# Pacing the top-k rounds of a sparse-attention indexer: two per group of products in place of four in three groups

## The chip, the cores and the metric

The kernel runs on one core of one Trainium2 chip. The metric is the device time of one execution in microseconds. The median of three runs is 1857.63 us (1857.12 to 1858.28).

## What is computed

Two layers of a causal decoder trunk on 512 tokens of width 1024, in float32. Each layer has a mixer with three branches and a convolutional GeGLU. Branch A is a dilated window attention, B an attention over the keys that an indexer selects, C a differential attention of four heads. All three start from one projection; gates weigh them, and an output projection follows. Only the indexer matters here:

```python
logits = jnp.einsum('bqhd,bsd->bqhs', qib, k_idx)
score = jnp.einsum('bqhs,bqh->bqs', jax.nn.relu(logits), wb) * (IDX_DIM ** -0.5)
score = jnp.where(kpos[None, None, :] <= qpos[None, :, None], score, -jnp.inf)
_, idx = lax.top_k(score, topk)          # topk = 128 of 512 keys
```

B then attends over the selected keys alone. For the first 128 queries every causal key is selected, so only three tiles of 128 queries need a selection, over 256, 384 and 512 keys.

## The kernel before

TensorE works in float32 split into a high and a low part, so every product is three matmuls (`mm3`, lines 88 to 90). Weights come in by DMA on SP's queue into `wr`, ScalarE casts the high part `wh` (line 81), VectorE subtracts to get the low part `wl` (line 82). There are two `wr` buffers and five each of `wh` and `wl`; the loader runs one or two units ahead (`w_ahead`).

The mixer is written as a sequence of units in the list `ORDER`: projections of A and the indexer, then C heads 0 to 2, the gates `ga` 0 to 3, C head 3, `ga` 4 to 7, B, and the remaining gates. A unit of A, B or C has four tiles of products, and after each tile the function `slot()` (line 328) is called once. So a **group** below is one block of products and the call of `slot()` that stands behind it, numbered from 1 in each layer. A call emits, in this order: work that came due, two of the 24 indexer score jobs while there are any, the stages of the attention chains that are in flight (S: scores and softmax on lines 470 and 472, T: transposes and their split on lines 477 and 81/82, V: the product with the values on line 488), and last the top-k steps.

A **round** of top-k (`topk`, line 742) takes an 8-wide buffer `m8` (tag "s"), finds the eight largest scores of each row (MAX8, line 745) and replaces them with a mark (MATCH_REPLACE8, line 746, with a small load of the match values). There are 16 rounds for each of the three tiles, and a closing TENSOR_SCALAR on line 748 turns the marks into a mask. All of it runs on VectorE. Below, T1.1 to T1.16 are the rounds of the tile with 256 keys (its scores lie in the buffer `m`), T2.1 to T2.16 those with 384 keys and T3.1 to T3.16 those with 512 (both in `u`). A step that finds a tile finished takes the place of a round.

Seen in the order in which the code emits it (layer 0): T1.1 is in group 12, T1.13 in 21. In group 22 the function `combine_a` (lines 596 to 616) joins the first pair of A's outputs; it takes three "s" buffers, on lines 599, 605 and 606, and stands ahead of T1.14. T1.16 is in group 23, T2.1 in 25, T2.11 in 32. The three chains of C head 0 start in groups 33, 34 and 35. Each takes "s" buffers for the row minima (line 470) and for `r2` (line 675), and stands ahead of the rounds of its group: T2.12 in 33, T2.13 in 34 (the second `combine_a` is in that group as well), T2.14 and T2.15 in 35. T2.16 is in 36. The chains of C head 1 start in 37, 38 and 39, and T3.1 and T3.2 are in 38, T3.3 in 39, T3.16 in 49. `chains_b`, which needs the masks, is called in group 57; it runs all steps that are left first. In layer 1 the counter `tick` starts with what layer 0 left in it.

The tag "s" has 20 buffers (line 41), handed out by a framework that also decides, from its own simulated time, in which order each engine gets its instructions: an instruction that is ready while its engine is free may overtake work that was emitted earlier.

Of the kernel before, what the change touches and what calls it, by code (L numbers as in the profile page):

```python
# [49 lines left out]
def tile_trunk(ctx, tc, x, positions, w_in, w_br_a, w_br_b, w_br_c, w_out, lam_q1, lam_k1, lam_q2, lam_k2,  # L50
# [269 lines left out]
    fly = [None, None]  # L320
    score_jobs = []
    topk_steps = []
    tick = [0]

    def later(f, lag=1):
        pending.append([lag, f])
# [1 line left out]
    def slot():  # L328
        now = []
        for e in list(pending):  # L330
            e[0] -= 1
            if e[0] <= 0:
                pending.remove(e)
                now.append(e[1])
        for f in now:
            f()
        for _ in range(2):
            if score_jobs:
                score_jobs.pop(0)()
        c0 = chains.pop(0) if chains else None  # L340
        c1, c2 = fly
        if c1 is not None:
            c1.T()
        if c0 is not None:
            c0.S()
        if c2 is not None:
            c2.V()
        fly[0], fly[1] = c0, c1
        if topk_steps:
            tick[0] += 4  # L350
            while tick[0] >= 3 and topk_steps:
                tick[0] -= 3
                if next(topk_steps[0], None) is None:
                    topk_steps.pop(0)

    def rope(v, nh, t0, nt=1):
# [42 lines left out]
    def proj_unit(l, u, perm, nh, idx=None):  # L399
# [8 lines left out]
        for t in range(NT):  # L408
            units = w_get(keys)
            acc = proj_tile(units, t, n)  # L410
            w_ahead(2)
            nc.scalar.copy(qr[:, t], acc[:, 0:384])
            if perm is not None:
                nc.sync.dma_start(perm[t * P:(t + 1) * P, :], qr[:, t, 256:384])
            if idx is not None:
                nc.scalar.copy(idx["kr"][:, t, 0:HD], acc[:, 384:448])
                nc.scalar.activation(idx["w"][:, t, :], acc[:, 448:456], AF.Copy, scale=float(8 ** -0.5))
            if t < NT - 1:
                slot()
# [285 lines left out]
    def index_q(l, qi):  # L705
        keys = [(l, "I", kk) for kk in range(4)]
        for t in range(1, NT):
            units = w_get(keys)
            acc = proj_tile(units, t, 512)
            w_ahead(2)  # L710
            qr = alloc([P, 512], F32, "sm")
            nc.scalar.copy(qr, acc)
            rope(heads(qr.unsqueeze(1)), 8, t)

            def go(t=t, qr=qr):
                tp = palloc("tp")
                for b in range(4):
                    nc.tensor.transpose(tp[:, b * P:(b + 1) * P], qr[:, b * P:(b + 1) * P], ident)
                c = slice((t - 1) * P, t * P)
                stack_q(qi[:, 0:8:2, c], qi[:, 1:8:2, c], tp.rearrange("p (b c) -> p b c", b=4))  # L720
            later(go, 2)
            if t < NT - 1:
                slot()
# [28 lines left out]
    def branch(l, gi, c0, c1, oTs, ys, first_term):  # L752
        kt = len(oTs)
        cpu = 8 // kt
        for c in range(c0, c1):
            wg, wb = w_get([(l, "gate", gi, c), (l, "br", gi, c0, c // cpu)])
            acc = palloc("mm")
            for k in range(KT):
                mm3(acc, (wg[0][:, k], wg[1][:, k]), (xh[:, k], xl[:, k]), k == 0, k == KT - 1)
            w_ahead(2)  # L760
            th = alloc([P, S], F32, "th")
            nc.scalar.activation(th, acc, AF.Tanh, scale=0.5)
            pb = palloc("mm")
            cs = slice((c % cpu) * P, (c % cpu + 1) * P)
            for k in range(kt):
                mm3(pb, (wb[0][:, k, cs], wb[1][:, k, cs]), (oTs[k][:, 0], oTs[k][:, 1]), k == 0, k == kt - 1)
            y = ys[c // 2][:, c % 2]
            if first_term:
                nc.vector.scalar_tensor_tensor(y, th, 1.0, pb, op0=ALU.add, op1=ALU.mult)
            else:  # L770
                nc.vector.scalar_tensor_tensor(th, th, 1.0, pb, op0=ALU.add, op1=ALU.mult)
                nc.vector.tensor_tensor(y, y, th, op=ALU.add)
            slot()
            yield c
# [265 lines left out]
```

## Time and profile before

| | |
|---|---|
| median of three runs | 1857.63 us |
| the profiled execution, its own time | 1860.71 us |
| its span, first to last instruction | 1858.9 us |
| instructions | 25416 |
| TensorE (PE) busy | 1834.1 us |
| VectorE (DVE) busy | 1155.1 us |
| ScalarE (ACT) busy | 867.7 us |
| mean granted TensorE clock | 0.996 |

The profile covers one execution. PE is matmuls, PEld weight loads, DVE VectorE, ACT ScalarE, POOL GpSimd, SP the queue that issues the DMAs. Times in the rows are us from the start of the span, means are ns. L745 is line 745 of the code. A granted clock of 1.00 is 2.4 GHz and one of 0.50 is 1.2 GHz; a value between is the mean over a stretch.

### The profile page before, as it was taken

How to read it: one execution, taken by the hardware profiler on the slowest of the kernel's cores; microseconds unless marked ns; L12 is line 12 of the kernel's file. 1: busy time of each engine (PE TensorE's matmuls, PEld its weight loads, DVE VectorE, ACT ScalarE, POOL GpSimd, SP SyncE). 2: the span in 40 equal slices, each digit the busy share in tenths (PEclk: the TensorE clock that was granted, in tenths of full speed). 3: DMA queues.
4: the chain of work that ended last, by engine and by line, in shares of the span. 5: the costliest groups of instructions: out<-in, count | busy, mean ns of one | idle time of the engine just before them, and what ended most of it. 6: DMA issues, size and time to landing. Idle time of an engine off the chain costs nothing.

```text
span 1858.9 us, 25416 instructions
## 1 busy us (share of the span) xinstructions
PE 1834.1 (99%) x9565; PEld 1607.4 (86%) x9565; DVE 1155.1 (62%) x2138; ACT 867.7 (47%) x1518; POOL 28.3 (2%) x53
## 2 busy tenths in 40 slices
PE   8999999999999999999999999999999999999998
PEld 6999989988889888888889999789888798888886
DVE  6687798665457666642367787885545566666332
ACT  5665654463335444432256756545533354444221
POOL 0000000000000000000000000000000000000000
PEclk9999999999999999999999999999999999999999
DMA  5333323233343333333433333232332443332241
GB/s 162 90 80 101 85 66 84 70 91 90 104 143 121 105 102 91 96 100 126 127 105 84 80 99 89 78 79 77 97 98 86 149 123 98 103 94 91 102 152 64
DMA packets 265173, 185.22 MB, mean 100 GB/s; under 512 B 14710, under 2 KB 238298, under 8 KB 265050
## 3 DMA queue, kind: packets, MB, share of 16 engines
q1 hardware_dynamic: 265050, 183.60, 33.8%
q8 instruction: 75, 1.23, 0.3%
q14 instruction: 48, 0.39, 0.1%
HBM read 171.99 MB, written 11.57 MB: 99 GB/s over the span
## 4 chain that ended last, share of the span: by engine, by line
PE 67%; issue 20%; DVE 7%; DMA 3%; ACT 2%; SPq 1%; POOL 0%; DVEq 0%; POOLq 0%; ACTq 0%
PE mm L88 16%; PE mm L89 16%; PE mm L90 16%; PE sc L88 2%; PE sc L89 2%; PE sc L90 2%; PE pv L488 2%; PE sc L396 1%; PE sc L397 1%; PE tp L477 1%; DMA wr<-in_w_in_dram 1%; DVE wl L82 1%; PE pv L89 1%; PE pv L88 1%; PE pv L90 1%
## 5 line engine op out<-in xcount | busy, mean ns | idle before, releaser
L82 DVE TENSOR_TENSOR wl<-wr,wh 128x1024 fp32r<-128x1024 f32 (+2 forms) x314 | 359.1, 1146 | 369.5 <-ACT wh L81 368.6
L81 ACT CAST wh<-wr 128x1024 fp32r<-128x1024 f32 (+2 forms) x314 | 309.4, 989 | 458.0 <-PE mm L90 135.5
L88 PE MATMUL mm<-xh,wh 128*128 128x512 f32 (+1 forms) x784 | 297.6, 380 | 1.3 <-ACT xh L81 0.8
L89 PE MATMUL mm<-xl,wh 128*128 128x512 f32 (+1 forms) x784 | 297.3, 379 | 0.0
L90 PE MATMUL mm<-xh,wl 128*128 128x512 f32 (+1 forms) x784 | 297.2, 379 | 0.0
L89 PE MATMUL mm<-wl,xh 128*128 128x384 f32 (+2 forms) x816 | 283.0, 348 | 0.9 <-DVE wl L82 0.9
L90 PE MATMUL mm<-wh,xl 128*128 128x384 f32 (+2 forms) x816 | 283.6, 348 | 0.0
L88 PE MATMUL mm<-wh,xh 128*128 128x384 f32 (+2 forms) x816 | 281.5, 348 | 1.3 <-ACT xh L81 0.7
L88 PEld LDWEIGHTS mm<-xh,wh 128*128 128x128 f32 x784 | 147.9, 189 | 27.8 <-ACT xh L81 1.2
L89 PEld LDWEIGHTS mm<-xl,wh 128*128 128x128 f32 x784 | 147.7, 188 | 26.2 <-DVE xl L82 0.4
L90 PEld LDWEIGHTS mm<-xh,wl 128*128 128x128 f32 x784 | 147.8, 188 | 26.1
L89 PEld LDWEIGHTS mm<-wl,xh 128*128 128x128 f32 x816 | 154.4, 189 | 5.7 <-DVE wl L82 1.9
L88 PEld LDWEIGHTS mm<-wh,xh 128*128 128x128 f32 x816 | 154.4, 189 | 5.7 <-ACT xh L81 1.7
L90 PEld LDWEIGHTS mm<-wh,xl 128*128 128x128 f32 x816 | 154.4, 189 | 4.0 <-DVE s L226 0.3
L90 PE MATMUL sc<-xh,wl 128*128 128x512 f32 (+1 forms) x272 | 99.2, 365 | 0.0
L89 PE MATMUL sc<-xl,wh 128*128 128x512 f32 (+1 forms) x272 | 99.0, 364 | 0.0
L88 PE MATMUL sc<-xh,wh 128*128 128x512 f32 (+1 forms) x272 | 98.8, 364 | 0.0
L88 PE MATMUL mm<-wh,qk 128*128 128x512 f32 x216 | 85.8, 397 | 0.0
L89 PE MATMUL mm<-wl,qk 128*128 128x512 f32 x216 | 85.4, 396 | 0.0
L90 PE MATMUL mm<-wh,qk 128*128 128x512 f32 x216 | 85.1, 396 | 0.0
L488 PE MATMUL pv<-v,pt 128*128 128x128 f32 (+1 forms) x280 | 71.2, 297 | 2.7 <-ACT pt L81 2.7
L472 ACT ACTIVATE sm<-sm,s 128x128 f32<-128x128 f32 (+2 forms) x96 | 53.5, 558 | 43.3 <-DVE s L470 43.1
(274 smaller groups left out, 3251.8 us busy)
## 6 DMA issues: line engine op xcount, KB each, us to landing
wr<-in_w_ffn_up_dram SPq DMA_DIRECT2D x176, 256.0 KB, 3.4
wr<-in_w_in_dram SPq DMA_DIRECT2D x282, 128.0 KB, 2.5
wr<-in_w_in_dram SPq DMA_DIRECT2D x56, 512.0 KB, 3.9
wr<-in_w_ffn_down_dram SPq DMA_DIRECT2D x44, 512.0 KB, 3.7
wr<-in_w_out_dram SPq DMA_DIRECT2D x16, 512.0 KB, 3.6
xd<-u SPq DMA_DIRECT2D x12, 512.0 KB, 3.7
u<-xd SPq DMA_DIRECT2D x12, 512.0 KB, 5.2
u<-in_x_dram SPq DMA_DIRECT2D x8, 512.0 KB, 5.9
```

Source lines behind the costliest of these rows:

```text
L81: nc.scalar.copy(hi, src)
L82: nc.vector.tensor_tensor(lo, src, hi.bitcast(F32), op=ALU.subtract)
L88: nc.tensor.matmul(dst, a[0], b[0], start=start, stop=False)
L89: nc.tensor.matmul(dst, a[0], b[1], start=False, stop=False)
L90: nc.tensor.matmul(dst, a[1], b[0], start=False, stop=stop)
L396: nc.tensor.matmul(dst, q, kh, start=True, stop=False)
L397: nc.tensor.matmul(dst, q, kl, start=False, stop=True)
L472: nc.scalar.activation(e, e, AF.Exp, bias=mneg, scale=-1.0, accum_out=dcol)
L477: nc.tensor.transpose(tp[:, b * P:(b + 1) * P], e[:, b * P:(b + 1) * P], ident)
L488: nc.tensor.matmul(dst, pT[0][:, c], v, start=i == 0, stop=False)
```

## The change

In `slot()` the counter `tick`, which gives four steps to three calls (one, one, two), is replaced by a loop that takes two steps in every call. Nothing else differs: the rounds, their widths and the chains are the same.

```diff
     topk_steps = []
-    tick = [0]
...
         if topk_steps:
-            tick[0] += 4
-            while tick[0] >= 3 and topk_steps:
-                tick[0] -= 3
-                if next(topk_steps[0], None) is None:
+            for _ in range(2):
+                if topk_steps and next(topk_steps[0], None) is None:
                     topk_steps.pop(0)
```

## Rows read from the trace of the kernel before

**Rows 1.** From the page: busy time of the engines over the whole span (share, number of instructions).

```profile
PE 1834.1 (99%) x9565; PEld 1607.4 (86%) x9565; DVE 1155.1 (62%) x2138; ACT 867.7 (47%) x1518; POOL 28.3 (2%) x53
```

**Rows 2.** The windows view: stretch and its length, busy time (and instructions) of PE, PEld, DVE, ACT and POOL, the granted TensorE clock, the busy share of the DMA engines, GB/s. The first row is from layer 0, the second from layer 1.

```profile
240.00:270.00 30.00, 27.82 (x147) 23.94 (x146) 28.86 (x70) 20.10 (x39) 1.02 (x1) 0.94 0.36 89
...
1170.00:1200.00 30.00, 27.05 (x124) 21.96 (x124) 25.51 (x63) 15.57 (x35) 1.02 (x1) 0.89 0.24 65
```

**Rows 3.** The chain of work that ended last, in layer 1 between 1176 and 1186 us: start, us, what.

```profile
1177.32 0.61 DVE s L745
...
1178.44 0.75 DVE u L746 x2
...
1181.75 0.59 DVE s L745
...
1183.12 0.48 DVE pt L82
...
1183.64 0.47 PE pv L489
```

**Rows 4.** The same chain in layer 0 between 260 and 267 us.

```profile
262.68 0.59 DVE s L745
...
264.51 0.66 DVE u L746
...
265.84 0.87 PE tp L477 x3
```

**Rows 5.** VectorE's instructions by line and shape over the whole span: count, busy us, mean ns of one, idle time before them.

```profile
L745 DVE MAX8 s<-u 128x8 f32<-128x512 f32 x32 | 21.9, 684 | 0.1
...
L746 DVE MATCH_REPLACE8 u<-s,u 128x512 f32<-128x512 f32 x32 | 21.6, 676 | 0.0
...
L745 DVE MAX8 s<-u 128x8 f32<-128x384 f32 x32 | 17.7, 553 | 0.3
L746 DVE MATCH_REPLACE8 u<-s,u 128x384 f32<-128x384 f32 x32 | 17.4, 543 | 0.0
...
L745 DVE MAX8 s<-m 128x8 f32<-128x256 f32 x32 | 13.6, 424 | 0.5
L746 DVE MATCH_REPLACE8 m<-s,m 128x256 f32<-128x256 f32 x32 | 13.1, 408 | 0.0
...
L746 DVE MATCH_VALUE_LOAD u<-s,u 128x8 f32 x64 | 5.6, 87 | 0.7
```

**Rows 6.** The timeline of VectorE in layer 0: start, us, engine, line, operation, out<-in. The MAX8 at 116.68 is that of T1.13; the next ones shown are those of T1.14, T2.11, T2.12, T2.13 and T3.2.

```profile
116.68 0.41 DVE L745 MAX8 s<-m 128x8 f32<-128x256 f32 x1
...
164.17 0.16 DVE L606 TENSOR_TENSOR s<-md,u 128x8 f32<-128x8 f32 x1
164.25 0.42 DVE L745 MAX8 s<-m 128x8 f32<-128x256 f32 x1
...
194.46 0.56 DVE L745 MAX8 s<-u 128x8 f32<-128x384 f32 x1
...
221.83 0.16 DVE L675 RECIPROCAL s<-s 128x2 f32<-128x2 f32 x1
221.91 0.54 DVE L745 MAX8 s<-u 128x8 f32<-128x384 f32 x1
...
234.56 0.55 DVE L745 MAX8 s<-u 128x8 f32<-128x384 f32 x1
235.03 0.67 DVE L470 CUSTOM_DVE_ANT_0 sm<-sc,cmask 128x512 f32<-128x512 f32 x1
...
265.61 0.69 DVE L745 MAX8 s<-u 128x8 f32<-128x512 f32 x1
266.22 0.67 DVE L470 CUSTOM_DVE_ANT_0 sm<-sc,cmask 128x512 f32<-128x512 f32 x1
```

**Rows 7.** The windows view of VectorE alone (stretch, length, busy time, instructions, granted clock, DMA share, GB/s): the stretch that ends where the first `combine_a` has taken its buffers, and the one from there to the end of the last wait of PE nearby; layer 0, then layer 1.

```profile
91.00:164.20 73.20, 57.64 (x143) 1.00 0.33 87
164.20:266.80 102.60, 85.95 (x218) 0.99 0.34 87
1009.00:1080.30 71.30, 56.38 (x143) 1.00 0.32 84
1080.30:1185.00 104.70, 88.71 (x221) 0.99 0.35 91
```

**Rows 8.** The windows view of the top-k lines alone (same columns), after those stretches: line 745 (first two rows), line 746 (next two), line 748 (last two), each time layer 0 and layer 1.

```profile
266.80:346.00 79.20, 9.58 (x14) 0.99 0.27 69
1185.00:1256.00 71.00, 9.29 (x14) 0.96 0.25 66
...
266.80:346.00 79.20, 11.26 (x30) 0.99 0.27 69
1185.00:1256.00 71.00, 10.51 (x28) 0.96 0.25 66
...
266.80:346.00 79.20, 0.42 (x1) 0.99 0.27 69
1185.00:1256.00 71.00, 0.43 (x1) 0.96 0.25 66
```

**Rows 9.** The windows view of all engines (columns as in Rows 2) in the two stretches where the rounds T1.1 to T1.13 stand closest.

```profile
91.00:117.20 26.20, 26.20 (x153) 25.98 (x153) 24.87 (x63) 16.95 (x32) 0.00 (x0) 1.00 0.31 79
...
1009.50:1037.00 27.50, 27.50 (x163) 27.28 (x162) 25.93 (x66) 17.17 (x33) 0.00 (x0) 1.00 0.30 81
```

## The prediction

> **What bounds the kernel now.** I read the page first. TensorE is busy for 1834.1 of 1858.9 us, VectorE for 62% [rows 1]. The change adds and removes no instruction, it moves the rounds of one VectorE loop to earlier places. So it can only move the 24.8 us in which TensorE is idle, and the time that it spends at the lower clock. Next I looked in the windows view for where TensorE idles in the part that the change touches. There is one place per layer that matters, at the passage from C's projections to the first gates: 2.18 of 30 us idle in layer 0 (30.00 less 27.82), 2.95 in layer 1 [rows 2]. In both the granted clock falls behind the idle time: its mean is 0.94 and 0.89, which is 30 x 0.06 = 1.8 and 30 x 0.11 = 3.3 us of full speed not granted, one of the two levels being half. The rest of TensorE's idle time lies mostly at the start and the end, out of reach.
>
> Third, the chain of waits says what those places wait for. In layer 1 it runs through VectorE, and three pieces of it are top-k: 0.61, 0.75 and 0.59 us, ahead of the split of `pt` on line 82 that TensorE's product waits for [rows 3]. In layer 0 there are two, 0.59 and 0.66 us [rows 4]. VectorE is not the bound of the kernel, but it is the bound of this place.
>
> Last, the timeline shows what decides where a round runs, and it is not only the group in which it is emitted. T1.13 runs at 116.68 us, well ahead of its group; then no round runs for 47 us, and T1.14 follows at 164.25, directly behind line 606, the third "s" buffer of `combine_a` [rows 6]. T1.14 is exactly the first round that the code emits behind `combine_a`. T2.11 runs at 194.46, T2.12 waits until 221.91, directly behind line 675 of C head 0, behind which it is emitted. So the "s" buffers are handed out in program order: rounds run ahead as filler until the next "s" user that isn't ready. It holds the other way round too: line 470 of head 0's third chain comes directly behind the MAX8 of T2.13 (234.56, 235.03), and that of head 1's third chain directly behind T3.2 (265.61, 266.22) [rows 6]. A chain of C can't start its softmax before every round emitted ahead of it has its buffer.
>
> **The change, part by part.** A round of 512 columns costs 684 + 676 + 87 = 1447 ns, of 384 columns 553 + 543 + 87 = 1183 ns, of 256 columns 424 + 408 + 87 = 919 ns [rows 5]. I counted the emission again with two steps per call: T1.16 is in group 19, T2.3 in 21, `combine_a` in 22 as before, T2.16 in 28, T3.8 in 32, T3.10 in 33, T3.12 in 34, T3.14 in 35, T3.16 in 36, where it was 49.
>
> *Ahead of `combine_a`.* T1.14 to T1.16 and T2.1 to T2.3 become free to run in the stretch that ends at 164.2 us: 3 x 0.92 + 3 x 1.18 = 6.3 us more, where VectorE idles for 73.2 less 57.64 = 15.6 us; in layer 1 for 14.9 [rows 7]. TensorE has no wait there. I cost it at nothing; the cover is that idle time, and if it failed the price would be the 6.3 us.
>
> *From there to TensorE's wait.* All of T3 now has to run before head 1's first chain, so what stood behind 266.8 us comes forward: 9.58 + 11.26 + 0.42 = 21.3 us in layer 0, 9.29 + 10.51 + 0.43 = 20.2 in layer 1 [rows 8]. Out of the stretch go the 6.3 us just counted (in layer 1 5.4, since its counter starts one round further on). Net 15.0 and 14.8 us more. VectorE idles there for 102.6 less 85.95 = 16.65 us, and for 104.7 less 88.71 = 16.0 us [rows 7]. Left after the change: 1.65 and 1.2 us, under 2%. How full can it get? The fullest stretches, with rounds at hand as filler all the time, still leave 26.2 less 24.87 = 1.33 us (5.1%) and 1.57 us (5.7%) [rows 9]. At these shares 5.2 us of 102.6 and 6.0 of 104.7 stay unfilled, so VectorE overruns by 5.2 less 1.65 = 3.6 us and 6.0 less 1.2 = 4.8 us, 8.4 us together. What of it reaches TensorE no row settles. Nothing, if what is late is work for later units: behind the stretch 21 us of VectorE come free. All, if it is the chains of C. In the stretches of [rows 9] VectorE was 94 to 95% busy and TensorE lost nothing; in the 30 us to 270 it was 96% busy and TensorE lost 2.18 us [rows 2]. One of each kind: I take half, 4.2 us.
>
> *The chains of C.* Ahead of head 0's third chain there is now a round of T3 and the MAX8 of the next, 1.45 + 0.68 = 2.1 us, in place of the MAX8 of T2.13, 0.55 us: 1.6 us later on a piece that was on the path [rows 5, 6]. Head 0's second chain gets the same. Against it stand the rounds that leave the last few us before TensorE's wait, 1.25 us in layer 0 and 1.95 in layer 1 [rows 3, 4]. The two nearly cancel, and both are inside the VectorE sum above, so I add nothing.
>
> *The clock.* The wait stays where it is and the clock falls as before: 0 on the sum. Bounds: both falls gone, 1.8 + 3.3 = 5.1 us less; one more fall of 1.8 us in each layer, 3.6 us more.
>
> *Behind the stretch.* VectorE is relieved of 21 us, but TensorE has no wait there that the windows show, so it gains nothing. The masks are needed only in group 57, long after. No DMA is moved; SP and POOL keep their order, except that a late `wl` gives its `wr` back later, which is in the overrun.
>
> Sum: +4.2 us. The profiled execution (1860.71 us, 1.8 us of it around the span, 3.1 above the median) would become 1864.9, the median 1857.63 + 4.2 = **1861.8 us**.
>
> One rule of the Trainium skill speaks against the forecast: "Perfetto Trace Analysis", section "Identifying the Most-Contended Engine", names the engine with the highest occupancy as the one to work on, and for VectorE takes occupancy as a fair measure. At 62% the move would cost nothing and the sum would be 0. The same page's section "Optimization Strategy" adds that kernels can have regimes in which another engine is the contended one; the windows of this trace agree with that (96% of VectorE in the 30 us to 270).
>
> **The rivals.** *A: filler stays filler, no change.* TensorE's matmuls do not depend on the rounds, the buffers hold weights one or two units ahead, and it lost nothing at 95% of VectorE [rows 9]. The rounds already run ahead of their groups, so the new pace changes little of what VectorE does when. Then the overrun falls on later work and the time is 1857.6, give or take 2. Against it: the order of the "s" buffers makes the rounds a condition for the chains of C. That the change does nothing because the buffers, not the pace, place the rounds would look the same; but the counted emission moves rounds past those users, so I hold it for a part of this case only.
>
> *B: faster.* The waits at the passage to the gates are made by the top-k rounds inside them. With T3 finished by about 255 us these rounds are gone, and the chain gets 1.25 + 1.95 = 3.2 us shorter; the idle time before the falls of the clock shrinks and with it half of their cost, 2.6 us. That is 5.8 us less: 1851.8. It decides for itself if T3.16 is through before head 1's first chain needs it, and if the overrun stays under 1.25 us. For it: the pieces of [rows 3, 4] are directly ahead of the wait. Against it: under 2% of idle time is left in the 100 us before.
>
> *C: all of the overrun lands on TensorE.* 8.4 us and another fall of the clock per layer, 3.6: +12, 1869.6. For it: the path already runs through VectorE there. It is the far end of my own case.
>
> **How the numbers follow.** A difference of 0.2%, 3.7 us, is about what a measurement of this kernel can tell from no change. My case, from +2 us to the far end C, holds 0.48; a part of it lies under 3.7 us. Rival A holds 0.30, rival B 0.22. So slower by over 0.2%: 0.41; within: 0.37 (A and the small end of my case); faster: 0.22 (B). My case alone gives 1859.5 to 1869.6. The range for 8 in 10 goes from 1852.8, which takes in half of B, to 1868.5, which leaves out the tip of C.
>
> **What would show it.** In the changed profile T1.16 should run before about 130 us, T2.4 should follow line 606 of the first `combine_a`, T3.9 line 675 of head 0's first chain, and T3.16 should stand ahead of line 470 of head 1's first chain, by 255 us. No top-k should stand behind 266 us or 1185 us. VectorE should be at 96 to 99% from 164 to 267 us and from 1080 to 1185. If I am right, TensorE's idle time in the two passages grows from 5.1 us to 7 to 13 us, or new waits on `wl`, `pt` and `sm` appear from 195 us on. If that idle time shrinks and no new wait appears, B is right and the step that failed is the share of the overrun that reaches TensorE. If the rounds don't keep to this order of "s" buffers, the count of what moves is wrong.

## The result: 1.3% slower, behind the predicted range

| | before | after |
|---|---|---|
| median of four runs each, same chip | 1857.38 us | 1882.8 us (1880.57 to 1884.07) |
| the profiled execution, its own time | 1860.71 us | 1882.3 us |
| its span | 1858.9 us | 1880.5 us |
| mean granted TensorE clock | 0.996 | 0.993 |

The ratio is 1.0130, with an interval of 1.0118 to 1.0143: 25 us slower, where 4 were forecast and the range ended at 1868.5. The sign was right, the size was not.

From the page after, the line of [rows 1]:

```profile
PE 1844.8 (98%) x9565; PEld 1610.2 (86%) x9565; DVE 1158.6 (62%) x2138; ACT 866.8 (46%) x1518; POOL 28.1 (1%) x53
```

The same instructions run, and VectorE is still at 62%. TensorE's idle time goes from 24.8 to 35.7 us. Where it lies, the windows view tells. First the kernel before, then the one after, over the two passages of [rows 2] made wide enough to hold them in both (columns as there):

```profile
240.00:290.00 50.00, 47.82 (x254) 41.46 (x253) 43.59 (x105) 30.47 (x61) 1.16 (x2) 0.97 0.29 75
1170.00:1220.00 50.00, 47.05 (x239) 40.84 (x239) 41.70 (x107) 25.65 (x60) 2.12 (x2) 0.93 0.23 61
```

```profile
240.00:290.00 50.00, 42.51 (x219) 35.47 (x218) 43.69 (x107) 31.08 (x66) 1.02 (x1) 0.93 0.21 53
1170.00:1220.00 50.00, 43.40 (x201) 35.75 (x200) 42.58 (x100) 29.81 (x61) 1.02 (x1) 0.83 0.21 53
```

Idle time in the two passages: 2.18 + 2.95 = 5.1 us before, 7.49 + 6.60 = 14.1 after. Full speed not granted: 50 x (0.03 + 0.07) = 5.0 us before, 50 x (0.07 + 0.17) = 12.0 after. That is 9.0 + 7.0 = 16.0 of the 21.6 us between the spans, and the page's idle time adds 1.9 from elsewhere. Some 3.7 us are in matmuls that show as busy and stay unplaced. Outside the passages little is lost: layer 1's first block of products ends 10.5 us later than before, and around the second passage another 11 us are added.

What TensorE waits for there, in layer 0 and then in layer 1 (waits of PE: its operation and line, the releaser, us, times, longest). First the longest wait in the kernel before, then the waits after:

```profile
PE pv L489 <- DVE pt L82: 0.9, 1, 0.9
...
PE pv L489 <- DVE pt L82: 1.3, 1, 1.3
```

```profile
PE sc L393 <- DVE s L467: 2.6, 1, 2.6
PE pv L485 <- ACT pt L81: 1.2, 1, 1.2
PE pv L486 <- DVE pt L82: 0.9, 1, 0.9
PE mm L90 <- DVE wl L82: 0.8, 1, 0.8
...
PE sc L393 <- DVE s L467: 3.6, 2, 2.4
PE pv L485 <- DVE th L522: 1.2, 1, 1.2
```

Lines of the kernel after are three lower than before: L467 is the softmax (L470), L603 `combine_a`'s third "s" (L606), L672 `r2` (L675), L742 and L743 the round (L745, L746), L382 and L383 the splits that prepare head 1's queries (L385, L386). The longest wait is TensorE's next scores waiting until the softmax has read the ones before. The timeline of VectorE after, for [rows 6] (T1.16, T2.4, T3.9, T3.11, T3.16 and the end of T3):

```profile
121.36 0.43 DVE L742 MAX8 s<-m 128x8 f32<-128x256 f32 x1
...
164.93 0.17 DVE L596 TENSOR_TENSOR s<-md,u 128x8 f32<-128x8 f32 x1 [2.49 <-DMA u<-ascr]
...
168.23 0.15 DVE L603 TENSOR_TENSOR s<-md,u 128x8 f32<-128x8 f32 x1
168.31 0.55 DVE L742 MAX8 s<-u 128x8 f32<-128x384 f32 x1
...
231.26 0.16 DVE L672 RECIPROCAL s<-s 128x2 f32<-128x2 f32 x1
231.33 0.67 DVE L742 MAX8 s<-u 128x8 f32<-128x512 f32 x1
...
240.56 0.16 DVE L603 TENSOR_TENSOR s<-md,u 128x8 f32<-128x8 f32 x1
240.63 0.69 DVE L742 MAX8 s<-u 128x8 f32<-128x512 f32 x1
...
247.09 0.68 DVE L382 TENSOR_TENSOR qk<-tp,qk 64x512 fp32r<-64x512 f32 x1
...
262.40 0.69 DVE L742 MAX8 s<-u 128x8 f32<-128x512 f32 x1
263.12 0.29 DVE L467 CUSTOM_DVE_ANT_0 sm<-sc,cmask 128x128 f32<-128x128 f32 x1
...
266.97 0.42 DVE L745 TENSOR_SCALAR u<-u 128x512 f32<-128x512 f32 x1
...
267.90 0.15 DVE L672 RECIPROCAL s<-s 128x2 f32<-128x2 f32 x1
```

Each of these rounds stands on the side of the "s" users that the counted emission gave it. What moved is the clock time of everything behind them. In the timeline before, the same landmarks are:

```profile
237.54 0.68 DVE L385 TENSOR_TENSOR qk<-tp,qk 64x512 fp32r<-64x512 f32 x1
...
257.60 0.16 DVE L675 RECIPROCAL s<-s 128x2 f32<-128x2 f32 x1
```

So VectorE is 4.1 us late at `combine_a` (164.17 to 168.23), 9.4 at head 0's first `r2` (221.83 to 231.26), 9.6 at head 1's queries and 10.3 at head 1's first `r2`. The delay is nearly full size at 231 us. TensorE's first wait of over 0.6 us in the passage comes 16 us later, its longest 39 us later (timeline of PE after):

```profile
247.21 0.36 PE L485 MATMUL pv<-v,pt 128*128 128x256 f32 x1 [0.64 <-DVE th L522]
...
270.49 0.50 PE L393 MATMUL sc<-qk 128*128 128x512 f32 x1 [2.65 <-DVE s L467]
```

In between TensorE's own order hides the delay. The framework plans all engines anew for each kernel, and it put the scores of C further back among the products. Those for the first of the two softmaxes of head 0's third chain stand here, before and after:

```profile
226.28 0.39 PE L396 MATMUL sc<-qk 128*128 128x512 f32 x1
```

```profile
236.82 0.39 PE L393 MATMUL sc<-qk 128*128 128x512 f32 x1
```

They come 10.5 us later, though TensorE has waited for next to nothing by then. The windows of VectorE, before and after, from the first `combine_a` to head 0's first `r2` and on to head 1's:

```profile
164.20:221.80 57.60, 45.78 (x114) 1.00 0.27 67
221.80:257.60 35.80, 31.01 (x81) 1.00 0.45 118
```

```profile
168.20:231.30 63.10, 58.49 (x141) 1.00 0.30 75
231.30:267.90 36.60, 34.27 (x85) 1.00 0.39 103
```

The first stretch grew by some 5.4 us (by its landmarks; the rounded ends give 5.5) and is 93% full, the second by 0.9.

### The profile page after: what moved, and what is told of

Read it like the earlier page. It is cut to its first block, busy times and chain, and to the rows that moved or that the text cites. A ratio compares the mean times of both kernels' runs of the same rounds, so it can differ in the third digit from the quotient of the medians.

```text
span 1880.5 us, 25417 instructions
## 1 busy us (share of the span) xinstructions
PE 1844.8 (98%) x9565; PEld 1610.2 (86%) x9565; DVE 1158.6 (62%) x2138; ACT 866.8 (46%) x1518; POOL 28.1 (1%) x53
## 4 chain that ended last, share of the span: by engine, by line
PE 82%; DVE 9%; DMA 4%; ACT 2%; issue 1%; SPq 1%; POOL 0%; DVEq 0%; POOLq 0%; ACTq 0%
PE mm L88 19%; PE mm L89 19%; PE mm L90 18%; PE sc L90 4%; PE sc L88 4%; PE sc L89 4%; PE pv L89 2%; PE pv L88 2%; PE pv L90 2%; DVE wl L82 2%; PE pv L485 1%; DVE u L743 1%; DVE s L742 1%; PE tp L474 1%; PE sc L393 1%
```

## The experiments

Each time is set against runs of the kernel before on the same chip. The third column below is the busy time of the top-k lines on VectorE between the first `combine_a` and head 1's first `r2`, layers 0 and 1. The fourth is when that `r2` starts in layer 0. The fifth is how long VectorE stood at the second `combine_a`, waiting for the DMA of its input (line 596 after), in both layers; a dash is under 0.8 us.

| kernel | median, against before | rounds ahead, us | head 1's `r2` | wait, us |
|---|---|---|---|---|
| before | 1857.4 | 21.7, 21.1 | 257.6 | 3.1, 1.8 |
| after | 1882.8, 1.0130 | 38.8, 38.9 | 267.9 | 1.4, 2.5 |
| e1 own buffers | 1864.6, 1.0038 | 25.5, 24.7 | 260.9 | 3.9, 4.2 |
| e2 rounds held | 1880.3, 1.0121 | 38.4, 37.7 | 266.5 | 1.6, 2.5 |
| e3 both orders by hand | 1882.0, 1.0134 | 38.8, 38.9 | 266.0 | 1.3, 2.8 |
| e4 T3 at the old pace | 1879.6, 1.0121 | 29.7, 31.3 | 263.2 | 4.2, - |
| e5 T3 narrow | 1871.7, 1.0078 | 25.9, 26.0 | 261.6 | 5.3, 5.1 |
| e6 T3 late | 1857.8, 1.0000 | 15.6, 15.7 | 255.8 | 1.7, 2.2 |
| e7 before, more load | 1866.8, 1.0048 | 30.1, 30.0 | 257.8 | 4.5, 3.3 |
| e8 three steps in two calls | 1868.4, 1.0053 | 24.2, 24.3 | 255.4 | 1.2, 4.4 |
| e9 last four held | 1876.5, 1.0100 | 32.6, 32.7 | 262.3 | 1.2, 2.7 |
| e10 narrow, own buffers | 1860.3, 1.0012 | 12.6, 11.9 | 250.5 | -, 1.5 |
| e11 before, T3 late | 1859.1, 1.0005 | 21.7, 21.8 | 256.6 | 3.2, - |
| e12 one step per call | 1863.0, 1.0025 | 14.9, 14.8 | 251.8 | 1.4, 3.7 |

**e1: the rounds get buffers of their own.** Based on after.

```diff
-    ... s=20, ...
+    ... s=16, m8=4, ...
-            m8 = alloc([P, 8], F32, "s")
+            m8 = alloc([P, 8], F32, "m8")
```

> The change, but the 8-wide buffers of the top-k rounds come from a tag of their own (4 buffers; "s" keeps 16 of its 20), so neither do rounds wait for the chains' small buffers nor chains for rounds. The emitted order of all five engines is then the same with either pace. Theory ring (the chains of C wait for rounds that were emitted ahead of them, because both draw on "s" in order; T3.16 holds head 1's first chain until 262 us, in place of 253): the loss is gone, 1850 to 1863 us, head 1's first softmax at 245 to 255 us, both half-clock stretches at 3.4 us or none. Rival load (VectorE is too full from 164 to 267 us with all of T3 in it): the rounds are still all ahead of 267 us, so most of the 25 us stays, 1872 to 1885.

1864.58 us, 1.0038 [1.0023, 1.0053]. With own buffers the old and the new pace give the same program on every engine, instruction by instruction, so the pace acts only through the ring of "s" buffers (the 20, handed out in turn). Most of the loss goes, not all; the time lies 1.6 us above the ring's forecast. It follows too that the kernel before would be this same program with own buffers: they are no remedy, they cost 0.4% against the shared ring at the old pace. In the timeline of VectorE T3.16 runs 35 us ahead of head 1's first softmax:

```profile
220.94 0.69 DVE L742 MAX8 m<-u 128x8 f32<-128x512 f32 x1
...
255.59 0.28 DVE L467 CUSTOM_DVE_ANT_0 sm<-sc,cmask 128x128 f32<-128x128 f32 x1
```

Rounds that the ring held back run ahead of `combine_a` now, in idle time: 31.1 us of them from 91 us on, against 18.0 after.

**e2: does a chain wait for rounds, or do rounds wait for a chain?** Own buffers as in e1, and each MAX8 is ordered behind the last "s" user of `combine_a` or `r2` (`order` only fixes their sequence on VectorE). The chains are free of the rounds.

```diff
...
+        held[0] = nc.vector.tensor_tensor(d2, ...)       # combine_a, and r2 likewise
...
-            nc.vector.max(m8, w)
+            mx = nc.vector.max(m8, w)
+            if held[0] is not None:
+                order(mx, held[0])
```

> As e1, but each MAX8 is ordered on VectorE behind the last "s" user emitted ahead of it (the third buffer line of combine_a, the reciprocal r2 of C's chains). So the rounds keep about the places that they have in the changed kernel, and VectorE carries the same load in the same stretch; only the chains no longer wait for rounds. Theory ring: most of the loss is gone, 1856 to 1868 us, head 1's first softmax ahead of T3.16. Rival load: as the changed kernel, 1876 to 1886 us.

1880.25 us, 1.0121 [1.0106, 1.0136]: nearly the whole loss without any chain bound to a round. The prediction's picture, that a chain can't start before the rounds emitted ahead of it, is not what costs. T3.16 even stands behind head 1's first softmaxes here, and its first `r2` still comes at 266.54, only 1.4 us sooner than after:

```profile
258.06 0.69 DVE L743 MAX8 m<-u 128x8 f32<-128x512 f32 x1
...
259.90 0.29 DVE L468 CUSTOM_DVE_ANT_0 sm<-sc,cmask 128x128 f32<-128x128 f32 x1
...
262.28 0.69 DVE L743 MAX8 m<-u 128x8 f32<-128x512 f32 x1
...
266.54 0.17 DVE L673 RECIPROCAL s<-s 128x2 f32<-128x2 f32 x1 [0.29 <-ACT sm L470]
```

The ring does its harm in the other direction: it keeps rounds out of the idle time ahead of `combine_a` and piles them up behind it.

**e3: the other half of the ring as well.** e2, and each softmax of C ordered behind the last MAX8.

```diff
...
+        if ring and last_max[0] is not None:
+            order(i, last_max[0])
```

> As e2, and in addition each softmax of C is ordered behind the last MAX8 emitted ahead of it: the two-way order of "s" put back by hand, with separate buffers. Theory ring: the loss is back, 1878 to 1886 us. If the number of buffers (16 in place of 20) or something else of e1 and e2 were what helps them, this one would be fast too, below 1868 us. Rival load: 1876 to 1886 us, as e2.

1881.95 us, 1.0134 [1.0117, 1.0151]. The order of the instructions on TensorE, VectorE and ScalarE is that of after, place by place, and so is the time. It overlaps with e2: the chains' waiting adds some 2 us (1.7 between the medians).

**e4: the fast pace for T1 and T2 alone.** T3 keeps four steps in three calls. The edit is shown against the kernel before; `done` counts the finished tiles.

```diff
-            tick[0] += 4
+            tick[0] += 4 if done[0] % 3 == 2 else 6
...
+                    done[0] += 1
```

> The shared "s" as in the changed kernel, two steps per call for the tiles with 256 and 384 keys, but four in three calls for the tile with 512. T3.16 is then emitted about five groups later, behind head 1's first chain. Theory ring: that chain waits for T3.12 or so only, and part of the loss goes: 1862 to 1876 us. Rival load: the load from 164 to 267 us falls by some four rounds of 1.45 us per layer, a quarter of what was added, so about three quarters of the loss stays: 1874 to 1880 us.

1879.61 us, 1.0121 [1.0105, 1.0136]: outside the ring's forecast and at the upper end of the load's. 8 to 9 us of rounds leave the front of head 1's first `r2`, which comes at 263.2 instead of 267.9, but they run inside head 1's own chains, and TensorE has one wait of 5.5 us there. VectorE also stood 4.2 us at `combine_a` for its DMA.

```profile
PE tp L534 <- DVE th L702: 5.5, 1, 5.5
```

**e5: the load of T3 without its order.** T3's rounds work on 128 of 512 columns. The selection over the other 384 is left out.

```diff
-            nc.vector.max(m8, w)
+            wr_ = w if w.shape[-1] < 512 else w[:, 0:128]
+            nc.vector.max(m8, wr_)
```

> The changed kernel, but the 16 rounds of the 512-key tile work on the first 128 of its 512 columns (this leaves out the selection over the other 384). Pace, number of rounds, emission and the order of the "s" buffers are as in the changed kernel; only VectorE has less to do, some 16 x 0.8 = 13 us per layer. By now two theories are left. Theory load (the stretch from 164 to 270 us has too little idle time of VectorE left): the loss goes, 1853 to 1864 us. Rival order (the new emission makes the scheduler put TensorE's work in a worse order, whatever the rounds cost): 1874 to 1884 us.

1871.72 us, 1.0078 [1.0061, 1.0095]: 14 us of the loss stay though the rounds' work ahead of head 1 is only 4 to 5 us a layer above that of before. So the place of the instructions costs too. VectorE's waits from 224 to 262 us:

```profile
DVE s L596 <- DMA u<-ascr: 5.3, 1, 5.3
DVE wl L82 <- ACT wh L81: 2.2, 3, 0.9
```

VectorE takes its instructions in order. It stood 5.25 us at `combine_a` for a DMA (until 238.35), with the third chain's softmax and head 1's queries queued behind: the scores for that softmax were done by 233.2, it ran at 240.57. In the kernel after, rounds fill most of that time (1.4 us). That this stand is what costs the 14 us is argued, not tried: e1 and e7 have stands of 3 to 4.5 us and lose less.

**e6: T3 only behind head 1's last chain.** T1 and T2 at two steps, T3 at four in three and not before group 41. The edit is shown against the kernel before; `calls` counts the groups.

```diff
-        if topk_steps:
-            tick[0] += 4
-            while tick[0] >= 3 and topk_steps:
+        third = done[0] % 3 == 2
+        if topk_steps and not (third and calls[0] < 41):
+            tick[0] += 4 if third else 6
+            while tick[0] >= 3 and topk_steps and not (done[0] % 3 == 2 and calls[0] < 41):
...
```

> Shared "s", two steps per call for the tiles with 256 and 384 keys as in the changed kernel, but the 512-key tile starts only in group 41, behind head 1's last chain, at four in three calls. Theory load: VectorE has in the stretch the load of before less T3.1 to T3.3, so the time is that of before or less: 1850 to 1859 us. Rival order: the early part of the emission is that of the changed kernel, 1864 to 1880 us.

1857.83 us, 1.0000 [0.9991, 1.0010]. The loss is gone, and so are the falls of the clock: the windows view shows full speed through both passages, with 1.18 us of idle time in each.

```profile
240.00:270.00 30.00, 28.82 (x162) 25.04 (x161) 25.93 (x58) 21.17 (x43) 1.04 (x1) 1.00 0.35 89
1160.00:1190.00 30.00, 28.82 (x157) 24.59 (x156) 25.10 (x57) 21.78 (x44) 1.02 (x1) 1.00 0.35 89
```

Here too `combine_a` is 2.9 us later than before (167.1), and it costs nothing. So that delay alone is harmless where the stretch behind it has room.

**e7: load alone, on the kernel before.** The MAX8 of each T2 round is issued twice: 16 x 0.553 = 8.8 us a layer.

```diff
+            if w.shape[-1] == 384:
+                nc.vector.max(m8, w)
```

> The kernel before, with each MAX8 of the 384-key tile issued twice into the same buffer: 16 x 0.55 = 8.8 us per layer more on VectorE between 165 and 255 us, with pace and buffer order of before. Theory load: a loss as in the earlier runs, where 9 to 14 us more per layer cost 9 to 11: here 5 to 9 per layer, 1868 to 1876 us. Rival order: 1855 to 1862 us.

1866.84 us, 1.0048 [1.0033, 1.0063], just under the forecast of the load theory. Load costs without any change of the pace, here 9.5 us for 17.7. VectorE is at 83.5 of 95.7 us (87%) in layer 0, where the kernel before has 76.8 of 93.4 (82%). TensorE's longest wait in layer 0 is of the same kind as after:

```profile
PE sc L396 <- DVE s L470: 3.7, 1, 3.7
```

**e8: a smaller change.** Three steps in two calls, 1.5 a call where before has 1.33 and after 2. The edit is against before.

```diff
-            tick[0] += 4
-            while tick[0] >= 3 and topk_steps:
-                tick[0] -= 3
+            tick[0] += 3
+            while tick[0] >= 2 and topk_steps:
+                tick[0] -= 2
```

> Three steps in two calls, between the two kernels (1.33 and 2). T3.1 moves three groups forward, so four or five rounds of T3 more fall ahead of 270 us, some 6 us per layer. Theory load: 1860 to 1870 us. Rival order: anything between 1852 and 1884, without relation to the load.

1868.42 us, 1.0053 [1.0038, 1.0068], within the load's forecast. But a quarter of the step costs 0.4 of the loss, and in layer 0 its trace shows no loss at head 1, whose first `r2` comes 2 us sooner than before (1.6 us later in layer 1, at 1177.2). One wait of 1.6 us in each layer stands behind the last round of T3. The one of layer 1:

```profile
1327.81 0.30 PE L396 MATMUL sc<-qk 128*128 128x128 f32 x1 [1.59 <-DVE qk L385]
```

The profiled execution is the fastest of the four and 4.0 us above that of before; where the rest of the 11 us between the medians lies no trace shows.

**e9: the last four rounds of T3 held.** After, but T3.13 to T3.16 not before group 41.

```diff
...
             for _ in range(2):
+                if done[0] % 3 == 2 and steps[0] >= 12 and calls[0] < 41:
+                    break
```

> The kernel after, but the last four rounds of T3 (T3.13 to T3.16) are not emitted before group 41, that is behind head 1's last chain of C; all the others keep the pace of two a call. What they cost where they stand: 4 rounds of T3 at about 1.2 us, so some 5 us a layer are taken from in front of head 1's first softmax, out of the 15 us that VectorE had too much in the two layers together. Theory 'the last rounds ahead of head 1's first chain are what counts': head 1's first softmax comes by 257 us, nothing falls in a bunch, 1857 to 1863. Theory 'load of the stretch in proportion': 10 of 25 us come back, 1870 to 1874. Theory 'head 0's third chain behind T3.12 is where the time goes': 1874 to 1880, because that stays.

1876.49 us, 1.0100 [1.0085, 1.0115]: the third forecast. Somewhat over a quarter of the loss goes, and head 1's first `r2` comes at 262.3 in place of 267.9. Head 0's first `r2` is still at 230.6 and its third at 247.8, against 231.3 and 248.5 after. The rounds right ahead of head 1's first chain are not the main part; most of the delay is there before them.

**e10: load and ring both away.** e5 and e1 together; again the selection over 384 of T3's 512 columns is left out.

> Both parts of the account taken away at once: T3's rounds work on 128 of 512 columns (the selection over the other 384 is left out), and the top-k's results have four buffers of a tag of their own, so that no chain of C stands behind a round and the pace has no hold on the order. Theory 'load and order, and nothing else': within 3 us of the kernel before, 1854 to 1860. If something else in the change costs time (the emission by itself, the rounds of T1 and T2 that come earlier), 1864 to 1872 remain.

1860.31 us, 1.0012 [1.0003, 1.0021], as forecast by "load and order". `combine_a` is 5.7 us later than before (169.8), head 0's first `r2` is on time (220.2), and the clock holds in the first passage:

```profile
240.00:270.00 30.00, 30.00 (x168) 26.36 (x167) 24.51 (x56) 20.52 (x42) 1.86 (x1) 1.00 0.36 88
1160.00:1190.00 30.00, 27.82 (x147) 24.33 (x146) 23.36 (x54) 19.04 (x39) 1.01 (x1) 0.94 0.35 89
```

With after, e1 and e5 it makes a table of two by two: 1.0130, without the ring 1.0038, with narrow rounds 1.0078, with both 1.0012. The ring is worth 0.9% at full width and 0.7% at narrow; it is the larger part. The rounds ahead of head 1 are not held equal in it: without the ring 25.5 us at full width and 12.6 at narrow, with it 38.8 and 25.9.

**e11 and e12: can the passage be relieved?** e11 is before with T3 not before group 41 (the condition of e6 at the old pace). e12 is before at one step per call. The first edit is shown against e6, the second against before.

```diff
-            tick[0] += 4 if third else 6
+            tick[0] += 4
```

```diff
-            tick[0] += 4
-            while tick[0] >= 3 and topk_steps:
-                tick[0] -= 3
+            tick[0] += 1
+            while tick[0] >= 1 and topk_steps:
+                tick[0] -= 1
```

> The kernel before with its own pace of four steps in three groups, but T3 is not begun before group 41, behind head 1's last chain of C. The first rounds of T3 (the trace of before has T3.1 and T3.2 by 266 us) leave the stretch, some 2 to 5 us of VectorE a layer. Theory 'rounds that stand ahead of head 1's chains cost time, rounds behind them none': equal to or faster than before, 1851 to 1857, with less of the 10 us at half clock that before has in its two passages. Theory 'before has enough room there': 1856 to 1859.

> The kernel before with one step in each group in place of four in three: the other side of the pace. In the stretch up to head 1's last chain VectorE has 10 to 12 rounds fewer, but rounds still stand between the chains and the last of T3 come 10 to 20 groups later. Theory 'load in front of head 1's chains': 1850 to 1857. Theory 'any round between the chains costs': same as before, 1856 to 1860. If something waits for the last round of T3 (the masks of the second part of the attention), slower than 1860.

e11: 1859.11 us, 1.0005 [0.9996, 1.0014], no difference; it was to be equal or faster, and its first two rounds of T3 ran behind head 1's first `r2` already in the kernel before. e12: 1863.02 us, 1.0025 [1.0014, 1.0036], slower, though VectorE has some 6.5 us a layer less ahead of head 1. The time is that of the third forecast, but no wait for the last round of T3 is in the trace. Rounds stand between the pieces of head 1's chains in place of ahead of them, and in layer 1 TensorE waits for the split of `pt`:

```profile
PE pv L489 <- DVE pt L82: 2.0, 1, 2.0
PE sc L396 <- DVE s L470: 1.1, 1, 1.1
```

The profiled execution is only 0.5 us above that of before, so most of the 4.6 us between the medians no trace shows. No version beats the kernel before; e6 and e11 equal it.

## Why the prediction was wrong

*Where the rounds go* was right. T1.16 ran at 121.36, T2.4 behind line 603 (168.31), T3.9 behind head 0's `r2` (231.33), and the net move of 15.0 and 14.8 us was measured as 14.2 and 13.5 (rounds up to head 1's last `r2`). Three signs failed: T3.16 came at 262.40, not by 255; in layer 1 T3 ended behind 1197.9, not by 1185; and VectorE was at 92% and 88% from 164.2 to 266.8 us and from 1080.3 to 1185, not at 96 to 99%. TensorE's idle time in the passages, 14.1 us, went just past the 7 to 13 named.

*"Ahead of `combine_a`: I cost it at nothing; if it failed the price would be 6.3 us."* It failed by 4.1 us. VectorE has idle time in that stretch, 77.2 less 63.6 = 13.6 us after, but not where A's last chains need it. TensorE did not wait for it, so the cost looked like zero there. It was carried on, because the stretch behind had too little idle time left to take it back. e6 and e10 have such a delay too (2.9 and 5.7 us) and a stretch with room, and have lost it by head 1's first `r2`.

*"From there to TensorE's wait", the step that failed.* It balanced 100 us as one sum, took the fill of [rows 9] as within reach, and gave half of the overrun to TensorE: 8.4 us for both layers, 4.2 taken. The runs show three faults. First, the sum has intermediate due times. From the first `combine_a` to head 0's first `r2` the rounds grew by 11.2 us (15.5 to 26.7) where 11.8 us were idle; the stretch got 5.4 us longer. Second, the fill. There it reached 93%, and over the whole stretch to head 1's last `r2` 93% and 90% in the two layers, not the 94 to 95% of [rows 9], where no attention chain goes back and forth between the engines; 7.4 and 10.9 us stayed idle, not 5.2 and 6.0. Third, the share. Late by 4.06 + 5.37 + 0.87 = 10.3 us on VectorE in layer 0 at head 1's first `r2` and by some 12.3 in layer 1 (less the 10.5 brought from layer 0), and TensorE came out 10.4 and 11 us later: all of it, not half. The share of VectorE from `combine_a` to head 1's first `r2` in layer 0 sorts most of the runs: 79 to 83% in before, e6, e10, e11 and e12, all within 5 us of before; 86 to 93% in e8, e4, e7, e1, e9, e2, e3 and after, which lose over 6 us. It is no limit that was tried: e5 loses 14 us at 84%, and e8, at 86%, has head 1's first `r2` sooner than before.

*"The chains of C: I add nothing."* In the sum that is near: e2 and e3 put the chains' waiting for rounds at some 2 us. But what a late head 1 does was missed. Its three `r2` come at 267.9, 272.1 and 275.9, in 8.0 us where they were spread over 14.3 (257.6, 262.5, 271.9). The gates' products that used to lie between the stages are spent by then (most run from 251 to 262 us, ahead of the second chain's scores), so each hand-over between TensorE and VectorE is open: the 2.65 us wait for the scores' buffer is one of them.

*"The clock: 0, bounds -5.1 and +3.6."* It cost 7.0 us, outside the bounds, and the idle time before it did not stay as it was.

*Rivals.* A (filler stays filler) holds for the pace by itself: with own buffers it changes nothing. With the ring the rounds are bound. B failed by its second condition: T3.16 was through before head 1's first softmax (262.40, 263.12), but the overrun was 10 us and not under 1.25. C named the right place and all of the overrun, 12 us; the overrun itself was mis-sized.

The Trainium skill's rule that the prediction weighed ("Perfetto Trace Analysis", section "Identifying the Most-Contended Engine") would have said 0: VectorE stands at 62% in both kernels while the time differs by 1.3%. The same page's section "Optimization Strategy", on regimes with other bounds, is the one that the windows bear out (VectorE at 93% from the first `combine_a` to head 1's first `r2`).

What stays open: every edit lets the framework plan all engines anew, so TensorE's order changes with the rounds' place. Some 2600 of the 9565 matmuls come from another line than at the same place before; only e3 has the order of after. No run holds that order fixed, so what it costs by itself is not shown. Against its being the cause, e6 and e10 differ from before about as much (some 2150 and 2730) and equal it. Open too is how much of e1's last 7 us is load and how much its long stands at `combine_a` (3.9 and 4.2 us); no run parts them. That the falls of the clock follow from the idle time was read from rows and not tried apart from it. Where e8 and e12 lose most of their time was not found.

## What to carry to other kernels

Filler work is free only up to the next due time of the engine that runs it: balance it stretch by stretch between due times, carry what is late from one into the next, and look where the engine is first late, which was here 39 us ahead of the longest wait of another one. A shared ring of buffers is an order of its own; it can keep filler out of the idle time that it was meant for and pile it up in front of a chain that matters. The same ring did no harm at the old pace, so it is the pace and the ring together that have to be looked at. Where an engine's work is a chain of hand-overs, don't count on the fill that it reaches elsewhere: here 90 to 93% with every late microsecond passed on, where 94 to 95% had been seen with no chain in flight.

## What the runs showed of the hardware

Behind the waits in the two passages of after TensorE was granted half of its speed for a while (1.2 of 2.4 GHz; 0.93 and 0.83 as means over 50 us). In e6, with 1.18 us of idle time in each passage, it kept 1.00 throughout. The clock's price was of the size of the waits themselves: 7.0 us more beside 9.0 us of added idle time. And VectorE did not go round an instruction that waited for a DMA: it stood 5.25 us in e5, while a softmax behind it, whose scores had been done by 233.2 us, ran only at 240.57.
